# Attention of a two-layer transformer trunk: where the maxima stand between the scores, and the reciprocal in two halves

## The chip, the cores and the metric

One core of a Trainium2 chip runs the whole kernel. The metric is device time in microseconds for one execution, the median of several runs. TensorE (PE) does the matmuls, VectorE (DVE), ScalarE (ACT) and GpSimd (POOL) the rest, SyncE (SP) issues the transfers.

## The reference

A trunk of two layers over 1024 latent tokens and 256 context tokens, 1024 wide. Layer 0 mixes tokens by grouped-query attention (16 heads of 64, 4 key heads), layer 1 by latent attention (16 heads, 96 wide for the scores, 64 for the values); each mixer is followed by a gated feed-forward part. What the change touches is the attention:

```
s = einsum('bqhgd,bkhd->bhgqk', q, k) * scale
p = softmax_f32(s)
o = einsum('bhgqk,bkhd->bqhgd', p, v)
```

Queries are the latent tokens, keys and values context and latent tokens (1280). In layer 0 the context tokens attend to themselves as well.

## The kernel before, in words

All matmuls of large operands are made of 2 or 3 passes over a high and a low part of each operand. Everything is transposed: channels or keys on the partitions, tokens in the columns.

Attention works in units: a pair of heads by 512 queries, 16 units per layer (and in layer 0 eight small context units of 256 queries on the side). A unit goes over the 1280 keys in ten blocks of 128. In `Attention.run` (line 789) each block k does this: `scores` (line 661) writes the scores of both heads, 512 columns each, into a two-bank PSUM tile `psD` (two of those); ScalarE's exponential writes them to a tile `pt` of 1024 columns; GpSimd adds `pt` to the unit's running sum (block 1 goes to VectorE); and after every second block `flush` (line 796) multiplies the `pt` of two earlier blocks by the values into a bank `psB`. Layer 0 has 2 passes per head in `scores`, layer 1 has 3.

The softmax needs a maximum for each query ahead of the unit's scores. `unit_max` (line 617) works it out: 20 steps per unit, each a 512-column matmul (or two of 256) into a bank `psB` and a `reduce_max` of that bank by VectorE. After the last step VectorE takes the maximum over the three parts (`m`), ScalarE and VectorE write its two 16-bit parts (`mm`), and `max_row` (line 650) turns them into two rows beside the queries, so that the next unit's scores come out with the maximum subtracted. The steps of a unit are spread over the blocks of the unit before and the one before that: behind each block, up to three steps are taken while their number is under what is due, which rises by two per block.

A finished unit goes through `tail` (line 688): the value sums are copied from their bank, two matmuls with a matrix of ones add up the running sum over the partitions into another bank `psB` (this is done at the head of the next flush), VectorE takes the reciprocal of that bank in place and multiplies it with the copied values (`s<-psB,s`), and the product is stored. Since TensorE's next maxima need VectorE to free their banks, `tail` sets `em.calm`: no step is taken for 2.8 us behind the reciprocal.

There are four banks `psB`. The maxima, the value sums, the sums for the reciprocal, the projections of queries and keys and the maximum rows all use them.

The order of the work is made on the host. A class `Emitter` holds a planned time `em.now`; each matmul adds its planned cost (in `mm`, 512 columns at 2400 per us plus 0.0135), and side tasks written as generators yield the planned time after which they go on. They run inside a matmul's tick, except in a flush, which is emitted alone (`em.alone`, line 144); what falls due in it follows behind it. Inside attention every engine keeps this order (`pinned`).

Of the kernel before, what the change touches and what calls it, by code (L numbers as in the profile page):

```python
# [25 lines left out]
EPS = 1e-6  # L26

MROW_WAIT = 5.0
CALM = 2.8
PO_WAIT = 0.3  # L30
PACE0 = 0.5
STEPS = 20
# [129 lines left out]
def build(ctx, tc, A, out):  # L162
# [17 lines left out]
    pe, act, dve, pool = Engine("pe", nc.tensor), Engine("act", nc.scalar), Engine("dve", nc.vector), Engine("pool", nc.gpsimd)  # L180
    em = Emitter()
# [29 lines left out]
    def s4(dt=F32):  # L211
        return bp.tile([P, 1024], dt, tag="s4", name=nm("s4"), bufs=8)
# [6 lines left out]
    def ptile():  # L219

        tag, pool_, n = ptags["order"][ptags["next"] % len(ptags["order"])]
        ptags["next"] += 1
        return pool_.tile([P, 1024], F32, tag=tag, name=nm("pt"), bufs=n)

    def s2(dt=F32):
        return bp.tile([P, 512], dt, tag="s2", name=nm("s2"), bufs=5)

    def pD():
        return ps.tile([P, 1024], F32, tag="D", name=nm("psD"), bufs=2)

    def pB():
        return ps.tile([P, 512], F32, tag="B", name=nm("psB"), bufs=4)
# [13 lines left out]
    def mm(o, l, r, start=True, stop=True, tp=None, more=False):  # L246

        n = r.shape[-1]
        if r.dtype == F32:
            c = max(4 * n, 4 * l.shape[-1]) / 2400.0 * (1.0 if tp is None else 0.5 if l.shape[-1] == 64 else 0.28)  # L250
        elif r.dtype == F32R:
            c = n / 2400.0 + em.over
        else:
            c = 0.06
        if tp is None:
            pe.matmul(o, l, r, start=start, stop=stop, skip_group_check=more)
        else:
            pe.matmul(o, l, r, start=start, stop=stop, tile_position=tp)
        em.tick(c)
# [81 lines left out]
    def mm3(o, wh, wl, xh, xl, first=True, last=True, more=False):  # L341
        mm(o, wh, xh, first, False, more=more)
        mm(o, wh, xl, False, False, more=more)
        mm(o, wl, xh, False, last, more=more)
# [313 lines left out]
        u["ready"] = True  # L658
        yield 0.0

    def scores(u, S, kc):
        nq = u["nq"]
        for h in range(2):
            passes = u["passes"][h]
            for j, (k, q) in enumerate(passes):
                mm(S[:, h * nq:(h + 1) * nq], k[:, kc * P:(kc + 1) * P], q, j == 0, j == len(passes) - 1)

    def weigh(u, po, pt, kc, first, last):
        nq = u["nq"]
        for h in range(2):  # L670
            mm(po[64 * h:64 * h + 64, :nq], u["v"](h, kc), pt[:, h * nq:(h + 1) * nq], first, last, tp=(0, 64 * h))
# [5 lines left out]
    def run_jobs():  # L677
        while jobs:
            jobs.pop(0)()

    def post(job):

        if gather[0]:
            jobs.append(job)
        else:
            job()

    def tail(u, po, acc):
        nq = u["nq"]
        yield PO_WAIT  # L690
        o = s2()
        act.copy(o[:, :nq], po[:, :nq])
        res = {}

        def total():
            pss = res["pss"] = pB()
            for h in range(2):
                mm(pss[64 * h:64 * h + 64, :nq], ones, acc[:, h * nq:(h + 1) * nq], tp=(0, 64 * h))

        post(total)  # L700
        while not res:
            yield 0.3
        yield 1.0
        r = res["pss"][:, :nq]
        dve.reciprocal(r, r)
        em.calm = em.now + CALM * nq / 512
        yield 3.5 * nq / 512
        dve.tensor_tensor(o[:, :nq], r, o[:, :nq], ALU.mult)
        yield 1.2
        u["out"](o[:, :nq])  # L710
        u["done"] = True

    def ctx_unit(make, scale):
# [11 lines left out]
        for i, kc in enumerate((8, 9)):  # L725
            S = pB()
            scores(u, S, kc)
            pt = t[:, 2 * nq * i:2 * nq * (i + 1)]
            act.activation(pt, S[:, :2 * nq], AF.Exp, scale=scale)
            pts.append(pt)  # L730
            yield 1.0
# [10 lines left out]
        while not res:  # L742
            yield 0.3
        yield from tail(u, res["po"], acc)

    class Attention:
# [42 lines left out]
        def run(self, extra=None):  # L789
            em.spawn(self.prep(1))  # L790
            pend, adds = [], []
            gather[0] = self.inside = True
            pinned.update(ENGINES)
            em.over = 0.0135

            def flush(n):
                with em.alone():
                    run_jobs()
                    for _ in range(min(n, len(pend))):
                        u, po, pt, i = pend.pop(0)  # L800
                        if i == 0:
                            po[0] = pB()
                        weigh(u, po[0], pt, i, i == 0, i == 9)
                        if i == 9:
                            em.spawn(tail(u, po[0], u["acc"]))

            def add(u, pt, i):
                if i == 0:
                    u["p0"] = pt
                    return  # L810
                eng = dve if i in (LASTDVE if u is self.units[-1] else ACCD) else pool
                if i == 1:
                    u["acc"] = s4()
                    eng.tensor_tensor(u["acc"], u.pop("p0"), pt, ALU.add)
                else:
                    eng.tensor_tensor(u["acc"], u["acc"], pt, ALU.add)

            for i, u in enumerate(self.units):
                while "ready" not in u:
                    if self.steps >= (i + 1) * STEPS:  # L820
                        em.until(lambda: "ready" in u)
                    elif not next(self.max):
                        em.until(lambda t=em.now: em.now > t)
                if i + 2 < self.n:
                    em.spawn(self.prep(i + 2), 1.0)
                if extra:
                    extra(i)
                po = [None]
                for k in range(10):
                    S = pD()  # L830
                    scores(u, S, k)
                    pt = ptile()
                    act.activation(pt, S, AF.Exp, scale=self.scale)
                    while adds:
                        add(*adds.pop())
                    adds.append((u, pt, k))
                    pend.append((u, po, pt, k))
                    for _ in range(3):
                        if (em.now >= em.calm and self.steps < (i + 1) * STEPS + STEPS // 2 + 2 * (k + 1)
                                and not next(self.max)):  # L840
                            break
                    if len(pend) == BATCH + LEAD:
                        flush(BATCH)
            add(*adds.pop())
            while pend:
                flush(BATCH)
            pinned.difference_update(ENGINES)
            em.over = 0.0
            gather[0] = False
            run_jobs()  # L850
# [70 lines left out]
    class Up:  # L921
# [61 lines left out]
        def step(self, c, n, k):  # L983
            s = self.st[c]
            wn, xn = self.PR[n]
            w = self.ops[c][wn]
            wh, wl = w[:, k * P:(k + 1) * P], w[:, 512 + k * P:512 + (k + 1) * P]
            first = k == 0
            if n in ("V1", "V2", "G1", "G2"):
                o = s["ct"][:, 0:256] if n[0] == "V" else s["ct"][:, 256:512]  # L990
                kk = k + xn
                em.until(lambda: self.norm.ready(NX, kk))
                mm3(o, wh, wl, self.H["hh"][kk][:, NX:NT], self.H["hl"][kk][:, NX:NT], first and n[1] == "1",
                    k == 3 and n[1] == "2")
                return
            if n == "P1" and first:
                s["d"] = pD()
                s["a"], s["b"], s["ct"] = s["d"][:, 0:512], pB(), s["d"][:, 512:1024]
            if n in ("P2", "Q1") and first:
                s["x"] = pB()  # L1000
            o = s["b"] if n in ("P5", "P3") else s["x"] if n in ("P2", "Q1", "Q2") else s["a"]
            em.until(lambda: self.need(xn, k))
            xh, xl = self.mov(xn, k)
            more = n in ("P6", "P7", "P4", "P3")
            mm3(o, wh, wl, xh, xl, first and not more and n != "Q2", k == 3 and n != "Q1", more)
# [80 lines left out]
        def ahead(self):  # L1086
# [9 lines left out]
            self.ops[0]["go"] = True  # L1096

        def run(self, tail):
            em.until(lambda: "go" in self.ops[0])
            ctx = self.full  # L1100
# [1030 lines left out]
```

## Time and profile before

| what | us |
|---|---|
| median of 3 runs | 3445.76 |
| lowest and highest of them | 3443.13, 3451.75 |
| the profiled execution's own time | 3444.86 |
| its span, first to last instruction | 3443.1 |

The profile is of one execution. Times in it count from its first instruction. A matmul's duration is longer than the distance to the next matmul, because they are pipelined; the distance is what counts for a sum. Since nearly all instructions are recorded from one helper line (L175), the rows are told apart by the tiles that an instruction writes and reads, as `mx<-psB` for a reduction of a bank into the table of maxima.

### The profile page before, as it was taken

The page shows a single profiled execution, that of the slowest core. Times are in us where ns is not written, and L with a number is a line of the kernel's source. Part 1 is how long each engine was busy: PE and PEld are TensorE (multiplying, and loading weights), DVE is VectorE, ACT ScalarE, POOL GpSimd, SP SyncE. Part 2 cuts the span into 40 slices and gives each one's busy share as a digit, 9 for nine tenths or more (in the row PEclk, how much of TensorE's full clock was granted, in tenths as well). Part 3 has the DMA queues.
Part 4 walks back from the last instruction along what each step waited for, and adds up shares of the span by engine and source line. Part 5 has one row for each costly group of instructions (what it writes and reads, how often), then busy time and mean ns, then how long its engine had stood idle before and what let it go on. Part 6 is the DMA issues. An engine that isn't in the chain of part 4 may idle for free. (4 is left out here: it accounts for less than half of the span.)

```text
span 3443.1 us, 41383 instructions
## 1 busy us (share of the span) xinstructions
PE 3204.6 (93%) x15482; PEld 2342.0 (68%) x15482; DVE 2134.5 (62%) x2577; ACT 1520.2 (44%) x2368; POOL 1909.7 (55%) x1128
## 2 busy tenths in 40 slices
PE   6999999999989999999899899999999899998998
PEld 4776445556778888878777555555557677776787
DVE  5355766763576676667764655555553776767585
ACT  4224555552344444444453444444442444444434
POOL 4324667774466666654443355555562656566455
PEclk9999999999999999999999999999999899999998
DMA  5645310002312222264231000000014122223633
GB/s 199 196 146 188 111 59 8 19 1 89 103 49 78 84 97 86 69 216 149 82 114 60 23 28 11 28 11 28 19 49 140 44 92 92 92 92 119 236 113 101
DMA packets 139050, 303.33 MB, mean 88 GB/s; under 512 B 15584, under 2 KB 35168, under 8 KB 138848
## 3 DMA queue, kind: packets, MB, share of 16 engines
q1 hardware_dynamic: 138848, 300.67, 26.2%
q8 instruction: 122, 2.00, 0.2%
q14 instruction: 80, 0.66, 0.1%
HBM read 224.85 MB, written 70.52 MB: 86 GB/s over the span
## 5 line engine op out<-in xcount | busy, mean ns | idle before, releaser
L175 POOL TENSOR_TENSOR s<-s,pt 128x1024 f32<-128x1024 f32 x248 | 594.6, 2398 | 257.1 <-ACT pt L175 238.2
L175 DVE TENSOR_REDUCE mx<-psB 128x1 f32<-128x512 f32 (+1 forms) x640 | 407.5, 682 | 247.8 <-PE psB L175 246.0
L175 PE MATMUL psD<-s,blk 128*128 128x512 f32 (+2 forms) x1600 | 453.3, 410 | 3.9 <-ACT s L175 2.7
L175 ACT ACTIVATE pt<-psD 128x1024 f32<-128x1024 f32 x320 | 327.0, 1023 | 293.8 <-PE psD L175 281.0
L175 PEld LDWEIGHTS psD<-s,blk 128*128 128x128 f32 (+2 forms) x1600 | 289.4, 191 | 179.4 <-issue 73.8
L175 PE MATMUL psD<-blk,wh 128*128 128x512 f32 (+1 forms) x1024 | 335.0, 403 | 9.6 <-ACT blk L175 4.0
L175 DVE SCALAR_TENSOR_TENSOR s<-s,par,s 128x1023 f32<-128x1023 f32 x176 | 291.5, 1670 | 68.4 <-ACT s L175 65.2
L175 PE MATMUL psB<-pt,blk 128*64 128x512 f32 x1280 | 323.2, 627 | 0.3 <-DVE s L175 0.3
L175 PE MATMUL psD<-blk,wlo 128*128 128x512 f32 (+1 forms) x1398 | 287.9, 354 | 30.9 <-POOL wlo L175 22.2
L175 PE MATMUL psD<-blk,pp 128*128 128x512 f32 (+1 forms) x1068 | 268.5, 395 | 19.9 <-ACT pp L175 10.8
L175 PEld LDWEIGHTS psD<-blk,wlo 128*128 128x128 f32 x1398 | 229.7, 190 | 78.1 <-POOL wlo L175 30.6
L175 PE MATMUL psB<-blk,s 128*128 128x512 f32 (+3 forms) x768 | 231.6, 384 | 45.2 <-DVE mx L175 33.9
L175 PE MATMUL psB<-blk,pp 128*128 128x512 f32 x1056 | 262.0, 396 | 3.6 <-DVE s L175 2.7
L175 DVE TENSOR_TENSOR s<-s,s 128x512 f32<-128x512 f32 (+3 forms) x193 | 197.2, 1024 | 89.5 <-ACT s L175 75.6
L175 DVE TENSOR_TENSOR pp<-pp 128x512 fp32r<-128x512 f32 (+1 forms) x165 | 145.4, 889 | 166.2 <-ACT pp L175 164.4
L175 PEld LDWEIGHTS psD<-blk,pp 128*128 128x128 f32 x1068 | 199.5, 191 | 63.8 <-ACT pp L175 12.1
L175 POOL TENSOR_TENSOR pp<-wraw,pp 128x512 fp32r<-128x512 f32 x88 | 144.9, 1647 | 171.8 <-ACT pp L175 171.8
L175 PEld LDWEIGHTS psD<-blk,wh 128*128 128x128 f32 (+1 forms) x1024 | 188.8, 189 | 74.7 <-issue 17.5
L175 POOL TENSOR_TENSOR s<-s,s 128x1024 f32<-128x1024 f32 (+4 forms) x72 | 143.8, 2001 | 170.0 <-ACT s L175 165.9
L175 PEld LDWEIGHTS psB<-blk,pp 128*128 128x128 f32 x1056 | 198.9, 191 | 50.6 <-DVE s L175 7.2
L175 PEld LDWEIGHTS psB<-blk,s 128*128 128x128 f32 (+1 forms) x768 | 141.3, 193 | 110.0 <-DVE mx L175 66.8
L175 POOL TENSOR_TENSOR whi<-blk,whi 128x512 fp32r<-128x512 f32 x97 | 143.8, 1483 | 127.8 <-ACT whi L175 123.1
(159 smaller groups left out, 6025.4 us busy)
## 6 DMA issues: line engine op xcount, KB each, us to landing
pp<-g SPq DMA_DIRECT2D x143, 256.0 KB, 2.8
g<-s SPq DMA_DIRECT2D x66, 512.0 KB, 2.7
s<-in_ada_w SPq DMA_DIRECT2D x48, 512.0 KB, 5.8
blk<-in_ada_w SPq DMA_DIRECT2D x48, 512.0 KB, 6.4
wraw<-in_w_up SPq DMA_DIRECT2D x88, 256.0 KB, 3.0
pp<-in_w_up SPq DMA_DIRECT2D x88, 256.0 KB, 3.9
blk<-in_w_dn SPq DMA_DIRECT2D x86, 256.0 KB, 3.4
wr<-in_w_out SPq DMA_DIRECT2D x16, 512.0 KB, 3.8
```

Of the source, the lines that this page charges most:

```text
L175: ins = fn(*a, **k)
```

## The change

In `scores` a function may be called between the two heads. `run` hands it one step of the maxima, if fewer than due less one are done. Behind the exponential's emission, in place of up to three steps, comes one step if fewer than due are done and a second if fewer than due less one are; and one more is possible behind a flush. A step is taken only when the planned time is past `em.calm`, as before. The reciprocal of 512 columns becomes two of 256 (the context units' of 256 stays one), each sets a calm of 1.0 us instead of 2.8 (1.4 for 256), and the task waits 2.3 planned us behind each instead of 3.5 (1.75) behind the whole.

```diff
 MROW_WAIT = 5.0
-CALM = 2.8
+CALM = 1.0
+RECW = 2.3
@@
-    def scores(u, S, kc):
+    def scores(u, S, kc, between=None):
         nq = u["nq"]
         for h in range(2):
+            if h and between:
+                between()
             passes = u["passes"][h]
             for j, (k, q) in enumerate(passes):
                 mm(S[:, h * nq:(h + 1) * nq], k[:, kc * P:(kc + 1) * P], q, j == 0, j == len(passes) - 1)
@@
         r = res["pss"][:, :nq]
-        dve.reciprocal(r, r)
-        em.calm = em.now + CALM * nq / 512
-        yield 3.5 * nq / 512
+        for a in range(0, nq, 256):
+            dve.reciprocal(r[:, a:a + 256], r[:, a:a + 256])
+            em.calm = em.now + CALM
+            yield RECW
         dve.tensor_tensor(o[:, :nq], r, o[:, :nq], ALU.mult)
@@
+            def step(due):
+                if em.now >= em.calm and self.steps < due:
+                    next(self.max)
+
             for i, u in enumerate(self.units):
@@
                     S = pD()
-                    scores(u, S, k)
+                    due = (i + 1) * STEPS + STEPS // 2 + 2 * (k + 1)
+                    scores(u, S, k, lambda: step(due - 1))
                     pt = ptile()
                     act.activation(pt, S, AF.Exp, scale=self.scale)
                     while adds:
                         add(*adds.pop())
                     adds.append((u, pt, k))
                     pend.append((u, po, pt, k))
-                    for _ in range(3):
-                        if (em.now >= em.calm and self.steps < (i + 1) * STEPS + STEPS // 2 + 2 * (k + 1)
-                                and not next(self.max)):
-                            break
+                    step(due)
+                    step(due - 1)
                     if len(pend) == BATCH + LEAD:
                         flush(BATCH)
+                        step(due)
```

## Rows read from the trace of the kernel before

**Rows 1.** The page's busy line, whole execution: busy us (share of the span) xinstructions.

```profile
PE 3204.6 (93%) x15482; PEld 2342.0 (68%) x15482; DVE 2134.5 (62%) x2577; ACT 1520.2 (44%) x2368; POOL 1909.7 (55%) x1128
```

**Rows 2.** Windows: length, busy PE, PEld, DVE, ACT, POOL, granted clock, DMA, GB/s.

```profile
290.00:805.00 515.00, 481.58 (x2228) 248.82 (x2229) 355.31 (x467) 277.91 (x396) 372.09 (x180) 0.98 0.18 63
1940.00:2540.00 600.00, 559.70 (x2449) 344.98 (x2449) 328.41 (x447) 258.92 (x369) 337.72 (x172) 0.96 0.07 22
2124.90:2130.00 5.10, 4.97 (x22) 2.85 (x23) 3.31 (x6) 2.48 (x4) 0.00 (x0) 1.00 0.00 0
2150.40:2153.80 3.40, 3.40 (x9) 1.04 (x9) 1.72 (x3) 0.00 (x0) 1.72 (x1) 0.50 0.00 0
```

**Rows 3.** The waits of TensorE's matmuls, 290 to 800 us: total, times, longest.

```profile
PE psB L175 <- DVE mx L175: 18.9, 32, 2.3
...
PE psB L175 <- DVE m L175: 1.8, 6, 0.4
```

**Rows 4.** The same view, 1940 to 2600 us.

```profile
PE psB L175 <- DVE mx L175: 22.3, 15, 2.9
PE psB L175 <- DVE blk L175: 7.8, 8, 1.2
PE psB L175 <- DVE s L175: 5.3, 4, 1.7
```

**Rows 5.** The timeline around the end of a flush: start, duration, idle before.

```profile
2137.67 1.91 PE L175 MATMUL psB<-pt,blk 128*64 128x512 f32 x8
...
2138.60 3.36 DVE L175 RECIPROCAL psB<-psB 128x512 f32<-128x512 f32 x1
...
2139.51 0.72 PE L175 MATMUL psD<-s,blk 96*128 96x512 f32 x2
```

**Rows 6.** The timeline of the same unit, 6 us later.

```profile
2144.87 7.25 POOL L175 TENSOR_TENSOR s<-s,pt 128x1024 f32<-128x1024 f32 x3
...
2145.89 0.85 PE L175 MATMUL psB<-blk,s 96*128 96x512 f32 x4
...
2146.32 1.29 DVE L175 TENSOR_REDUCE mx<-psB 128x1 f32<-128x512 f32 x2 [3.64 <-PE psB L175]
...
2146.58 1.56 PE L175 MATMUL psD<-s,blk 96*128 96x512 f32 x6
2147.64 0.18 DVE L175 TENSOR_REDUCE m<-mx 128x8 f32<-128x24 f32 x1
...
2147.97 0.63 PE L175 MATMUL psB<-blk,s 96*128 96x512 f32 x2
2148.10 1.63 DVE L175 SCALAR_TENSOR_TENSOR mm<-m,mm 128x8 bf16<-128x8 f32 x1 [0.28 <-ACT mm L175]
...
2150.38 0.80 PE L175 MATMUL psB<-blk,s 96*128 96x512 f32 x1 [1.78 <-DVE mx L175]
...
2151.11 3.27 PE L175 MATMUL psB<-pt,blk 128*64 128x512 f32 x8
```

**Rows 7.** The timeline of a unit of layer 1 with values to prepare.

```profile
2057.34 3.37 DVE L175 RECIPROCAL psB<-psB 128x512 f32<-128x512 f32 x1
...
2061.49 1.09 PE L175 MATMUL psB<-wh,blk 128*128 128x256 f32 x4 [1.66 <-DVE s L175]
```

**Rows 8.** Groups of VectorE instructions (busy, mean ns), and one tile's durations (min/median/max).

```profile
L175 DVE RECIPROCAL psB<-psB 128x512 f32<-128x512 f32 x32 | 107.4, 3355 | 35.5 <-PE psB L175 34.5 <-ACT s L175 0.9
L175 DVE RECIPROCAL psB<-psB 128x256 f32<-128x256 f32 x7 | 12.3, 1758 | 0.3 <-PE psB L175 0.2
L175 DVE TENSOR_REDUCE mx<-psB 128x1 f32<-128x512 f32 x240 | 155.5, 679 | 61.0 <-PE psB L175 60.1
L175 DVE SCALAR_TENSOR_TENSOR mm<-m,mm x40: 150/882/2248, 238.2 to 2563.5; 128x8 bf16<-128x8 f32 x32, 128x4 bf16<-128x4 f32 x8
```

**Rows 9.** The timeline of a unit of layer 0, around its reciprocal.

```profile
605.20 3.35 DVE L175 RECIPROCAL psB<-psB 128x512 f32<-128x512 f32 x1
...
608.47 0.62 DVE L175 TENSOR_REDUCE mx<-psB 128x1 f32<-128x512 f32 x1
```

## The prediction

> **What bounds the kernel now.** I read the page's busy line first: TensorE is busy for 93% of the span and no other engine for more than 62% [rows 1], so time is lost or won where TensorE waits or is slow. Two stretches hold everything the change touches, the attention of layer 0 (290 to 805 us) and of layer 1 (about 1900 to 2600 us). The windows view gives their granted clock [rows 2]: 0.98 and 0.96 of full speed, and 0.50, that is 1.2 instead of 2.4 GHz, in the 3.4 us that follow one wait. Over the 600 us of the second row 0.04 are 24 us lost to the clock; one drop of 3.4 us at half speed loses 1.7 us, so there are some thirteen drops.
>
> Next I read whom TensorE's matmuls waited for. In layer 0 it is the maxima on VectorE: 18.9 us in 32 waits, and 1.8 us for the final maximum [rows 3]. In layer 1 the maxima stand for 22.3 us in 15 waits, and a VectorE operation on "s" for 5.3 us in 4, the longest 1.7 us [rows 4]. The timeline shows what one of them is [rows 5, 6]. The planner bans maxima for 2.8 us behind the reciprocal, then lets three go behind each block, here four matmuls from 2145.89 on (two whole steps and one of two halves). The last maximum of the unit ends with a tiny VectorE operation "mm" on 8 columns that takes 1.63 us here, because it ends (2149.73) as GpSimd's running add ends. The reductions behind it are late, no PSUM bank is free, and the matmul at 2150.38 has waited 1.78 us. Behind it come the eight value matmuls in 3.27 us, at 1.2 GHz [rows 2, 6]; the same eight take 1.91 us at full clock [rows 5]. In a unit in four it looks different [rows 7]: the whole reciprocal (3.37 us) stands before the last maxima, and the wait is 1.66 us for the product "s" behind it. So an event costs 1.78 + 1.7 = 3.5 us; 27.6 us of waits in layer 1 are room for at most fifteen, and I count twelve, one for each drop but one. At stake in layer 1: 12 x 3.5 = 42 us.
>
> **The change, part by part.** It removes nothing but the three steps in a row. No matmul, DMA or queue is added or moved; what moves is where 20 maxima per unit stand in TensorE's and VectorE's order, and each of 32 full reciprocals becomes two.
>
> The halves. A 512-column reciprocal takes 3355 ns, one of 256 columns (the context units have them already) 1758 ns [rows 8]: 2 x 1758 - 3355 = 161 ns more per unit, 32 times, 5.2 us of VectorE. VectorE works 355 of 515 us in layer 0 and 328 of 600 in layer 1 [rows 2], and I cost this at nothing; without that cover it is 5.2 us. [...]
>
> The order, by the planner's costs (0.227 us for a 512-column matmul; 1.71 us for a flush, in which nothing else is emitted). Call F the end of the flush in the fourth block of a layer-1 unit; the tail emits the reciprocal 1 us behind it. New order: maximum 19 between the heads of the fifth block, half A, maximum 20 (the unit's last, with "mm") between the heads of the sixth, 21 behind it, flush. Half B is due at 1.13 + 2.3 = 3.4 us, inside the flush, so it is emitted behind that, bans maxima for 1 us, and 22 and 23 follow behind the seventh block, 24 between the heads of the eighth. Two per block, never three.
>
> Now with measured times, F = 2139.51 [rows 5]: six score matmuls take 1.39 us (2146.58 to 2147.97), the flush 1.84, a reduction starts 0.43 after its matmul and takes 0.68 [rows 6, 8]. Reduction 19 ends at F + 1.8; half A, which starts 2.7 us later than the reciprocal today (2138.60, F - 0.9), F + 3.6; reduction 20 F + 4.3; "mm" is ready 0.46 after the final maximum starts, at F + 4.7. GpSimd runs its adds back to back; one ends at 2144.87 = F + 5.4 [rows 6], and "mm" slips in there. Reduction 21 ends at 6.1, half B at 7.9, reduction 22 at 8.6. Matmul 24 is wanted at F + 7.9 and needs the bank of 22: two of the four banks of "psB" are held by the value sum and by the reciprocal's sums until the product. It waits 0.7 us where one waited 1.78: 12 x 1.08 = 13 us gained. The waits of up to 1.2 us on "blk" in layer 1 [rows 4] leave the clock where it was: behind one of them, from 2124.9 on, 1.00 was granted [rows 2]. So a wait of 0.7 should keep it; as the units with weights to prepare may differ from this one, I count nine of twelve, 9 x 1.7 = 15.3 us. Bounds for layer 1: all twelve stay (0) and all waits and drops go (27.6 + 20.4 = 48 us); nearest is the timetable. What is late next behind this wait is the exponential that gives the score tile back: a maximum between the heads delays it by 0.23 us, and ScalarE, busy 259 of 600 us [rows 2], hides that.
>
> Layer 0. A block has 4 score matmuls, so the fifth and sixth are through sooner and half B's ban reaches over the seventh. One maximum goes between A's block, none till the eighth, then eleven in three blocks. Today the reciprocal starts at 605.20, and one maximum waits behind it and is reduced at 608.47 [rows 9]. In the new order nothing stands between the halves, and A starts behind the maximum. But the steps are split by heads and flush, and where three follow a block today, blocks away from a reciprocal get two. I take half of 18.9 + 1.8, 10 us; bounds 0 and 20.7. The clock's 0.02 x 515 = 10 us I leave, bounds 0 and 10.
>
> Later ends. The product comes at 2 x 2.3 instead of 3.5 planned us, 1.1 later; behind each layer's last unit the projection starts with other units' outputs, so nothing waits.
>
> **Sum:** 13 + 15.3 + 10 = 38 us off the profiled execution's 3444.86 us: 3406.6. That execution lies 0.9 us below the median 3445.76, so 3407.
>
> **Rivals.** A, slower: "mm" misses the gap at F + 5.4 and waits for the next add, 2.4 us on. In place it decides all: reduction 21 ends at 8.5, matmul 23 waits 1.5 us for it; half B and reduction 22 follow at 10.9, matmul 24 waits another 1.5. That is 3.0 in place of 1.78, with the drop kept: 16 x 1.2 = 19.5 us more in layer 1, and half that in layer 0: 3445 + 29 = 3474. The margin is 5.4 - 4.7 = 0.7 us; against it speaks that the boundary repeats with the unit, for it that "mm" ranges from 150 to 2248 ns [rows 8]. [...]
>
> B, no change: the same wait appears one block earlier, with the same length, since the bank shortage stays: 3441, within 10 us of before.
>
> C, it doesn't do in layer 0 what it says: no maximum falls between half A and half B there, VectorE is held by both as by the whole, and nothing is won: 38 - 10 = 28 us, 3417.
>
> **The numbers.** Chances: forecast 0.50, A 0.14, B 0.14, C 0.22. A measurement of this kernel can tell about 0.3%, 10.3 us. Forecast and C are faster (0.72), B the same (0.14), A slower (0.14). The range goes from all of layer 1's and layer 0's waits gone with twelve drops (48 + 20.7 = 69, 3377) to B's far edge (3445.8 + 10.3 = 3456); A lies outside. The forecast and C alone span 3377 to 3430.
>
> **What would show it.** Right: layer 1's granted clock near 0.99; matmul waits on maxima there under 12 us; halves of 1.76 us with a reduction between them in layer 1; no block with three maxima in a row behind its scores. Wrong: "mm" at 1.6 us or more with a TensorE wait behind it in most units, the clock still 0.96, or new waits of the score matmuls on the exponentials.

## The result, and the profile of the changed kernel

The changed kernel takes 3405.49 us (median of 4 runs, 3404.28 to 3410.3), the kernel before 3444.45 us (4 runs, 3430.03 to 3451.75). The ratio on record is 0.9902 with the interval 0.9882 to 0.9921; the quotient of the two medians is 0.9887 and lies inside it. The total is the forecast's to within 2 us. Its split is not, as the windows show.

The head of the page and its busy line, after:

```profile
span 3402.8 us, 41374 instructions
...
PE 3169.4 (93%) x15482; PEld 2333.4 (69%) x15482; DVE 2163.1 (64%) x2609; ACT 1517.1 (45%) x2368; POOL 1902.4 (56%) x1128
```

Against [rows 1], VectorE has 32 instructions more (2609 for 2577), the second halves, and TensorE is 35.2 us less busy with the same 15482 matmuls. Most of that is its clock: the mean granted clock of the execution was 0.970 before and 0.977 after, and 0.007 of 3443 us are 24 us.

The windows from the first to the last exponential of each layer's attention and the stretch between them, first of the kernel before, then of the changed one (length, busy PE, PEld, DVE, ACT, POOL, granted clock, DMA, GB/s):

```profile
289.00:793.30 504.30, 474.05 (x2206) 245.68 (x2208) 345.69 (x460) 277.19 (x393) 366.53 (x179) 0.98 0.19 64
793.30:1953.90 1160.60, 1099.24 (x5633) 920.13 (x5630) 747.18 (x867) 513.98 (x867) 599.35 (x399) 0.97 0.28 95
1953.90:2595.00 641.10, 600.54 (x2609) 364.56 (x2609) 347.64 (x457) 278.30 (x385) 375.88 (x186) 0.96 0.08 26
```

```profile
289.70:805.70 516.00, 474.11 (x2212) 244.32 (x2212) 376.04 (x478) 275.67 (x393) 361.68 (x179) 0.98 0.19 64
805.70:1961.80 1156.10, 1095.06 (x5631) 920.47 (x5632) 746.94 (x867) 514.08 (x867) 595.97 (x399) 0.98 0.28 94
1961.80:2556.40 594.60, 572.65 (x2603) 359.26 (x2603) 345.29 (x471) 276.06 (x385) 376.22 (x186) 0.99 0.08 28
```

Layer 1 gained 641.1 - 594.6 = 46.5 us. Of these, 18.6 us are idle time of TensorE (length less busy: 40.6 before, 22.0 after) and 27.9 us busy time. Layer 0 **lost** 516.0 - 504.3 = 11.7 us, all of it idle time (30.3 before, 41.9 after) at an unchanged clock. The stretch between gained 4.5 us, whose cause was not sought. The sum is 39.3 us of the 40.3 us between the two profiled executions (3444.86 and 3404.57).

The inner part of layer 1 in the windows view of the changed kernel:

```profile
1980.00:2500.00 520.00, 505.13 (x2335) 320.09 (x2334) 306.75 (x428) 240.02 (x342) 329.04 (x165) 1.00 0.07 24
```

The clock is 1.00 there: none of the twelve drops to a granted 0.50, of which [rows 2] show one, is left. Two longer drops stand outside this row, at the ends of the layer (granted 0.50 from 1964.8 to 1971.6 us and from 2507.5 to 2514.3). The prediction's 1.2 and 2.4 GHz can be estimated, as columns per ns, from starts in the kernel before. In the drop of [rows 2] two pairs of value matmuls start at 2152.02 and 2152.87 us, 0.85 us for 1024 columns: 1.2. At full clock twelve matmuls of 512 columns take 2.72 us (1213.31 to 1216.03) and twelve of 256 right behind them 1.43 (to 1217.46), so 3072 columns more take 1.29 us more: 2.4. Below, TensorE's waits after, in layer 0 (290 to 800 us; total, times, longest) and in layer 1 (1965 to 2600 us):

```profile
PE psB L176 <- DVE mx L176: 28.4, 33, 3.0
```

```profile
PE psB L176 <- DVE mx L176: 13.4, 18, 4.4
PE psB L176 <- DVE blk L176: 5.7, 4, 2.1
PE psB L176 <- DVE s L176: 2.2, 4, 0.6
```

The waits on maxima rose in layer 0 from 18.9 to 28.4 us [rows 3]. In layer 1 they fell from 22.3 to 13.4 us [rows 4], of which one wait, at 2509 us in the last unit but one, is 4.4 us.

**Layer 1: the timetable held.** The timeline of a layer-1 unit after, with F = 2095.35 as the end of the flush in its fourth block (start, duration, idle before):

```profile
2095.35 0.96 PE L176 MATMUL psD<-s,blk 96*128 96x512 f32 x3
...
2096.59 0.69 DVE L176 TENSOR_REDUCE mx<-psB 128x1 f32<-128x512 f32 x1 [3.03 <-PE psB L176]
...
2097.19 1.75 DVE L176 RECIPROCAL psB<-psB 128x256 f32<-128x256 f32 x1
...
2098.51 4.88 POOL L176 TENSOR_TENSOR s<-s,pt 128x1024 f32<-128x1024 f32 x2 [1.75 <-ACT pt L176]
...
2098.86 0.63 DVE L176 TENSOR_REDUCE mx<-psB 128x1 f32<-128x512 f32 x1
...
2099.98 0.92 DVE L176 SCALAR_TENSOR_TENSOR mm<-m,mm 128x8 bf16<-128x8 f32 x1 [0.28 <-ACT mm L176]
...
2100.82 0.68 DVE L176 TENSOR_REDUCE mx<-psB 128x2 f32<-128x512 f32 x1
...
2101.42 1.75 DVE L176 RECIPROCAL psB<-psB 128x256 f32<-128x256 f32 x1
...
2103.09 1.21 DVE L176 TENSOR_REDUCE mx<-psB 128x1 f32<-128x512 f32 x2
...
2104.22 0.68 DVE L176 TENSOR_TENSOR s<-psB,s 128x512 f32<-128x512 f32 x1
2104.36 0.50 PE L176 MATMUL psB<-blk,s 96*128 96x512 f32 x1 [0.20 <-DVE mx L176]
```

"mm" is ready at F + 4.6 and ends at F + 5.55, as the first of the two adds in GpSimd's row ends (2098.51 plus half of 4.88 is 2100.95). So it still ends with an add, but sooner: it takes 0.92 us where it took 1.63 [rows 6]. Matmul 24 waits 0.20 us where one waited 1.78.

**Layer 0: the bank of the sums came back too late.** The timeline of the layer-0 unit of [rows 9], after:

```profile
607.19 1.08 PE L176 MATMUL psB<-s,ones 128*64 128x512 f32 x4
...
611.38 0.69 DVE L176 TENSOR_REDUCE mx<-psB 128x1 f32<-128x512 f32 x1 [1.73 <-PE psB L176]
...
611.99 1.76 DVE L176 RECIPROCAL psB<-psB 128x256 f32<-128x256 f32 x1
...
613.73 7.31 POOL L176 TENSOR_TENSOR s<-s,pt 128x1024 f32<-128x1024 f32 x3
613.78 2.60 DVE L176 TENSOR_TENSOR blk<-blk,blk 64x256 fp32r<-64x256 f32 x1
...
616.30 1.75 DVE L176 RECIPROCAL psB<-psB 128x256 f32<-128x256 f32 x1
...
618.64 0.50 PE L176 MATMUL psB<-blk,s 128*128 128x512 f32 x1 [1.50 <-DVE mx L176]
...
619.08 1.98 DVE L176 SCALAR_TENSOR_TENSOR mm<-m,mm 128x8 bf16<-128x8 f32 x1 [0.28 <-ACT mm L176]
...
621.58 0.67 DVE L176 TENSOR_TENSOR s<-psB,s 128x512 f32<-128x512 f32 x1
621.81 0.47 PE L176 MATMUL psB<-blk,blk 128*128 128x256 f32 x2 [0.80 <-DVE mx L176]
```

Read it as the life of one of the four "psB" banks. The sums are written into it from 607.19 on, and only the product that ends at 622.25 gives it back: 15.1 us. Before it was 6.5 us in this unit, from 603.30 to 609.82, with the reciprocal in between at 605.20 [rows 9]:

```profile
603.30 1.08 PE L175 MATMUL psB<-s,ones 128*64 128x512 f32 x4 [0.19 <-DVE mx L175]
...
609.13 0.69 DVE L175 TENSOR_TENSOR s<-psB,s 128x512 f32<-128x512 f32 x1
```

After, half A stands behind the next block's maximum, which TensorE delivers late (1.73 us idle). Between the halves comes a subtraction of 64x256, which takes 2.60 us and ends (616.38) about as GpSimd's first add of three does (613.73 + 7.31/3 = 616.17). Then half B, the last maximum and "mm", which ends (621.06) as the third add does (621.04); the product stands last. TensorE waits for a bank twice, 1.50 and 0.80 us.

This is no accident of one unit. Of the 31 "mm" of 128x8 in the two layers, 16 took over 0.7 us before and 23 after, and each of these 39 ended within 0.04 us of the end of a GpSimd instruction. The seven subtractions that took over 0.7 us after ended 0.28 to 0.29 us behind one. What ties these ends to each other was not shown.

The groups view of VectorE in layer 0 (290 to 805 us; busy, mean ns), before and then after, gives the sums:

```profile
L175 DVE SCALAR_TENSOR_TENSOR mm<-m,mm 128x8 bf16<-128x8 f32 x15 | 7.8, 518 | 4.2 <-ACT mm L175 4.2
L175 DVE TENSOR_TENSOR blk<-blk,blk 64x256 fp32r<-64x256 f32 x11 | 4.6, 419 | 0.1
```

```profile
L176 DVE TENSOR_TENSOR blk<-blk,blk 64x256 fp32r<-64x256 f32 x11 | 18.0, 1640 | 0.2
L176 DVE SCALAR_TENSOR_TENSOR mm<-m,mm 128x8 bf16<-128x8 f32 x15 | 16.1, 1073 | 4.5 <-ACT mm L176 4.5
```

The same eleven subtractions went from 419 to 1640 ns each, "mm" from 518 to 1073 ns: 13.4 + 8.3 = 21.7 us more of VectorE for the same work in another order.

### The profile page after: what moved, and what is told of

Read it like the earlier page. It is cut to its first block, busy times and chain, and to the rows that moved or that the text cites. A ratio compares the mean times of both kernels' runs of the same rounds, so it can differ in the third digit from the quotient of the medians.

```text
span 3402.8 us, 41374 instructions
## 1 busy us (share of the span) xinstructions
PE 3169.4 (93%) x15482; PEld 2333.4 (69%) x15482; DVE 2163.1 (64%) x2609; ACT 1517.1 (45%) x2368; POOL 1902.4 (56%) x1128
## 5 line engine op out<-in xcount | busy, mean ns | idle before, releaser
L176 POOL TENSOR_TENSOR s<-s,pt 128x1024 f32<-128x1024 f32 x248 | 592.4, 2389 | 224.9 <-ACT pt L176 126.5
L176 DVE TENSOR_REDUCE mx<-psB 128x1 f32<-128x512 f32 (+1 forms) x640 | 420.7, 682 | 228.4 <-PE psB L176 226.3
L176 PE MATMUL psD<-s,blk 128*128 128x512 f32 (+2 forms) x1600 | 483.3, 408 | 4.5 <-ACT s L176 3.3
L176 PE MATMUL psD<-blk,wlo 128*128 128x512 f32 (+1 forms) x1398 | 287.2, 353 | 31.0 <-POOL wlo L176 22.3
L176 PE MATMUL psB<-pt,blk 128*64 128x512 f32 x1280 | 311.0, 607 | 2.4 <-ACT pt L176 1.0
L176 PE MATMUL psB<-blk,s 128*128 128x512 f32 (+3 forms) x768 | 263.2, 381 | 30.1 <-DVE mx L176 21.7
L176 PE MATMUL psD<-blk,pp 128*128 128x512 f32 (+1 forms) x1068 | 268.6, 395 | 21.3 <-ACT pp L176 12.0
```

Of the source, the lines that this page charges most:

```text
L176: ins = fn(*a, **k)
```

## The experiments

"Layer 0" and "layer 1" below are the times from the first to the last exponential of each layer's attention in the profiled execution; before they are 503.3 and 640.1 us, after 515.0 and 593.6. Two profiles of a layer with the same order differ by up to some 6 us, as shown below, so smaller differences of these times are not read as effects. The kernel before took 3437.36 us beside the first four kernels (12 runs), 3439.6 beside the next four (7 runs) and 3439.12 beside the last two (7 runs).

### Which of the two parts does it, and in which layer

**The new places alone.** The maxima stand as in the change; the reciprocal is whole again, with its old ban and wait.

```diff
-CALM = 1.0
+CALM = 2.8
@@
-        for a in range(0, nq, 256):
-            dve.reciprocal(r[:, a:a + 256], r[:, a:a + 256])
-            em.calm = em.now + CALM
-            yield RECW
+        dve.reciprocal(r, r)
+        em.calm = em.now + CALM * nq / 512
+        yield 3.5 * nq / 512
```

> The new places of the maxima with the whole reciprocal of before and its calm of 2.8. Theory S (the three steps in a row make layer 1's waits and clock drops): layer 1's attention, 640 us before and 594 after, is at most 605, its granted clock 0.98 or more, and the kernel 3405 to 3415. Rival H (the halves let maxima through): layer 1 stays at 630 to 640 with 0.96, and the kernel within 10 us of before. Both: layer 0 tells whether the halves or the places cost the 12 us there, 503 against 515 us from the first exponential to the last.

Measured: 3406.82 us, ratio 0.9909 (0.9894 to 0.9923); layer 0 507.7, layer 1 598.0. That is the change's total, without the halves. Between 1980 and 2500 us it leaves two drops of the clock, near 2212 and 2369 us, where a matmul waits for the product behind a whole reciprocal, as in [rows 7]. The timeline and the window behind the first of them:

```profile
2211.95 2.63 PE L176 MATMUL psB<-wh,blk 128*128 128x256 f32 x12 [1.68 <-DVE s L176]
```

```profile
2212.50:2216.00 3.50, 3.50 (x16) 2.65 (x17) 1.23 (x4) 0.86 (x3) 2.82 (x2) 0.53 0.20 75
```

The halves end these two in the change (the waits on "s" are 2.2 us there, none over 0.6), which is some 4 us of layer 1, and layer 0 is 7.3 us longer with them. In the kernel's time the two nearly cancel. In layer 0 the halves move TensorE's waits from the product to the maxima: with the whole reciprocal (289.6 to 798.4 us) they are

```profile
PE psB L176 <- DVE mx L176: 14.6, 19, 3.6
PE psB L176 <- DVE s L176: 9.6, 8, 3.2
```

and with the halves 28.4 us on maxima and 1.4 us on "s".

**The halves alone.** The order of the maxima is the old one, up to three behind each block; the reciprocal is the change's. The edit, against the kernel before:

```diff
-CALM = 2.8
+CALM = 1.0
+RECW = 2.3
@@
-        dve.reciprocal(r, r)
-        em.calm = em.now + CALM * nq / 512
-        yield 3.5 * nq / 512
+        for a in range(0, nq, 256):
+            dve.reciprocal(r[:, a:a + 256], r[:, a:a + 256])
+            em.calm = em.now + CALM
+            yield RECW
```

> The two halves with calm 1.0 and 2.3 us behind each, but up to three steps behind each block as before. Theory S: layer 1 keeps most of its drops, clock 0.96 to 0.97, attention 625 to 640 us, the kernel 3430 to 3445. Rival H: layer 1 at 594 to 605 us, the kernel 3405 to 3415.

Measured: 3424.85 us, ratio 0.9963 (0.9948 to 0.9978); layer 0 516.7, layer 1 614.7 at a clock of 0.99 (1.00 between 1980 and 2470 us). Neither expectation holds as written. The halves alone take the drops away too and win 25.4 of 46.5 us in layer 1; they cost 13.4 us in layer 0. So the two parts don't add up: either one keeps the clock in most units of layer 1, and the old order keeps waits that the new one doesn't have (20.3 us on maxima in layer 1 against 13.4). The trace gives the reason why the halves alone do it. The durations of layer 1's "mm" (shortest, median, longest in ns), before and with the halves alone:

```profile
L175 DVE SCALAR_TENSOR_TENSOR mm<-m,mm x15: 171/1615/1626, 1977.8 to 2563.5; 128x8 bf16<-128x8 f32 x15
L176 DVE SCALAR_TENSOR_TENSOR mm<-m,mm x15: 170/209/2012, 1986.9 to 2543.9; 128x8 bf16<-128x8 f32 x15
```

The old order still lets three maxima follow a block, but half of the "mm" take 209 ns or less, where half took 1615 or more, and the waits on maxima are shorter: 28 of 0.7 us on average where before 15 of 1.5 us stood. The waits for the product, too, are 2.2 us with none over 0.6, as in the change.

**The change in layer 1 only, and in layer 0 only.** A flag, set as each attention starts, picks the old or the new order and reciprocal. Only the line that sets it is shown; 0.125 is layer 0's scale.

```diff
+            newway[0] = self.scale != 0.125
```

> The whole change in layer 1, layer 0 as before. Theory: layer 0's part is a loss of its own, 12 us, so 3405 - 12 = 3393, faster than both kernels. Rival: what layer 0 loses in attention comes back behind it (the stretch from its end to layer 1 was 4.5 us shorter after), so 3400 to 3405.

Measured: 3395.94 us, ratio 0.9874 (0.9859 to 0.9889); layer 0 504.5, layer 1 593.2.

```diff
+            newway[0] = self.scale == 0.125
```

> The whole change in layer 0, layer 1 as before. Theory: 12 us slower than before, 3452 to 3460, and layer 1's clock 0.96 as before. Rival (layer 1 gains because its start is shifted, not by its own order): layer 1 at 600 us here too, and the kernel under 3425.

Measured: 3448.7 us (9 runs), ratio 1.0027 (1.0015 to 1.0039); layer 0 514.1, layer 1 638.3. That is 11.3 us over the kernel before beside it, for 12 expected. The two layers can be told apart cleanly: layer 1's part alone is faster than the whole change, and layer 0's part is a loss of its own.

### What makes the events of layer 1

**The kernel before without VectorE's "mm".** The old order and the whole reciprocal stay. "mm" splits the negated maximum into two 16-bit columns, ScalarE the first, VectorE the rest. Here ScalarE writes half of it into both, and VectorE does nothing.

```diff
-        act.mul(mb[:, :w, 0], m[:, :w], -1.0)
-        dve.scalar_tensor_tensor(mb[:, :w, 1], m[:, :w], -1.0, mb[:, :w, 0], ALU.mult, ALU.subtract)
+        act.mul(mb[:, :w, 0], m[:, :w], -0.5)
+        act.mul(mb[:, :w, 1], m[:, :w], -0.5)
```

> The kernel before, with the tiny VectorE operation on mm replaced: ScalarE writes minus half the maximum into both 16-bit columns, so that their sum is the maximum rounded to 16 bits. The shift is a little coarser, which softmax does not see. Theory M (the wait of mm for GpSimd's add makes nine of the twelve events of layer 1): those nine go, three drops with the reciprocal stay; layer 1's attention falls from 640 to 605 to 618 us, and the kernel by 20 to 35 us. Rival S (three steps in a row are enough by themselves to run out of banks): waits of about 1 us stay in each unit, drops go or stay, layer 1 at 625 or more, the kernel within 15 us of before.

Measured: 3393.1 us, ratio 0.9864 (0.9849 to 0.988); layer 0 494.0, layer 1 604.0. This one edit is worth 46 us, more than the change and more than the 20 to 35 expected (layer 1 gains 36.1 us, and layer 0, which the theory left out, 9.3); and it leaves the three steps in a row where they were. TensorE's waits in layer 1 of this kernel (1940 to 2600 us):

```profile
PE psB L175 <- DVE blk L175: 8.7, 8, 1.2
PE psB L175 <- DVE s L175: 5.3, 4, 1.7
...
PE psB L175 <- DVE mx L175: 3.4, 4, 2.9
```

The waits on maxima went from 22.3 to 3.4 us, and the granted clock to 0.99; the waits on "blk" and "s" stayed about as in [rows 4]. Of the twelve drops two are left, near 2202 and 2363 us, behind waits for the product (up to 1.7 us). This shows what the prediction read from [rows 6]: the three steps were not the trouble by themselves, but a tiny operation in VectorE's queue ahead of two reductions. That it is long because it waits for a GpSimd add is read from the ends of the long ones, as above; no run moved the adds instead.

**The same edit on the kernel that has the change in layer 1 only.**

> The change in layer 1 alone (3396 us) and also ScalarE writing both 16-bit columns, in both layers. Theory: in layer 1 mm ran 0.8 to 0.9 us and its wait was hidden, so little is left there (0 to 5 us); in layer 0 the waits on maxima behind mm (1.8 us of TensorE waits on m, and part of 18.9 on mx) shrink by 3 to 8 us: 3384 to 3393. Rival (mm sets nothing any more): 3393 to 3398.

Measured: 3387.6 us, ratio 0.9845 (0.9828 to 0.9861); layer 0 488.4, layer 1 592.4. In layer 1 the edit gives 0.8 us more beside the new order (593.2 without it): both remove the same events. In layer 0, where the old order still has waits behind "mm", it gives 16.1 us here and 9.3 us in the kernel before. Both have the same order there, so two single profiles of a layer can differ by some 6 us.

### What costs in layer 0

**The reciprocal first.** The new places, the whole reciprocal as in the first experiment, and it is emitted without the planner's microsecond behind the sums.

```diff
             yield 0.3
-        yield 1.0
         r = res["pss"][:, :nq]
```

> The new places with the whole reciprocal (3407 us, layer 0 508 us), but the reciprocal is emitted at the end of the flush, ahead of the next block's maximum. Theory B (layer 0 loses because the reciprocal now stands behind a maximum of the next block, and its bank of sums is held the longer): layer 0 at 498 to 504 us, the kernel 3395 to 3403. Rival (the order of the reciprocal and that maximum is of no weight; the places themselves cost): layer 0 at 506 to 510 us, the kernel 3404 to 3409.

Measured: 3382.47 us, ratio 0.9833 (0.9813 to 0.9853); layer 0 486.4, layer 1 594.2. Layer 0 gains 21.3 us over the first experiment, more than the theory expected (498 to 504 us). The timeline of the same unit as above in this kernel:

```profile
587.64 1.08 PE L176 MATMUL psB<-s,ones 128*64 128x512 f32 x4
...
590.02 3.36 DVE L176 RECIPROCAL psB<-psB 128x512 f32<-128x512 f32 x1
...
594.40 0.69 DVE L176 TENSOR_TENSOR s<-psB,s 128x512 f32<-128x512 f32 x1
```

The reciprocal starts 2.4 us behind the first matmul of the sums, where half A started 4.8 us behind it (611.99 - 607.19), and the bank is back after 7.45 us (595.09) instead of 15.1. Over the sixteen units of layer 0 the mean of that time is 13.6 us in the change, 11.6 with the new places alone and 8.3 here, in the order of layer 0's times (515.0, 507.7, 486.4).

The bank's time is not all, though. In the kernel before its mean is 7.6 us, the shortest of these, and layer 0 takes 503.3 us. So with the bank held for about as long the new places win 16.9 us in layer 0 (503.3 to 486.4); the reciprocal's late start takes back 21.3 and the change's halves on top of it 7.3 more. The halves in the old order agree: 11.8 us and 516.7, where the new places have 507.7 at 11.6. In layer 1 a longer hold cost nothing that can be seen: its mean is 11.6 us in the change and 6.5 here, for 593.6 and 594.1 us.

**Both halves, back to back.** The change, but with no wait between the halves and the old ban and wait behind them.

```diff
-            em.calm = em.now + CALM
-            yield RECW
+        em.calm = em.now + 2.8 * nq / 512
+        yield 3.5 * nq / 512
```

> The change, but the second half stands right behind the first on VectorE, with the calm of 2.8 us and the 3.5 us of the whole behind both. Theory G (the 7 us that the change loses in layer 0 against the same places with a whole reciprocal come from the gap between the halves, in which other VectorE work slips in and the bank of sums stays held): layer 0 at 506 to 510 us, the kernel 3404 to 3410, as with the whole reciprocal. Rival F (a fixed cost of two instructions): layer 0 at 513 us or more.

Measured: 3406.45 us, ratio 0.9905 (0.9884 to 0.9926); layer 0 508.3, layer 1 597.0, within 1 us of the whole reciprocal in the same places (507.7 and 598.0). To split the instruction costs nothing that can be seen; what the halves cost in layer 0, they cost through the gap between them, or through the shorter ban on maxima that goes with it: this edit takes both back, and no run tells them apart. Each side was profiled twice: 515.0 and 514.1 us with the gap, 507.7 and 508.3 without.

**The halves first.** The change itself without the planner's microsecond (the same line goes as above).

> The change, with the first half emitted at the flush's end, ahead of the next block's maximum; the second 2.3 planned us later, calm 1.0 behind each. Theory: with the first half early the product still waits for the second, so layer 0 lies between 486 us (whole, first) and 515 (the change): 490 to 505, the kernel 3385 to 3398. Rival (the halves let maxima through, as they are meant to): layer 0 at 486 us or less and the kernel at 3382 or less.

Measured: 3396.07 us, ratio 0.9881 (0.9862 to 0.99); layer 0 507.3, layer 1 594.4. Started early, the halves are still 20.9 us longer in layer 0 than the whole reciprocal started as early (486.4), and longer than the 490 to 505 us expected. So the two prices don't add up either: over 486.4 us the late start alone costs 21.3 us, the halves alone 20.9 and both together, in the change, 28.6. The medians of the two kernels lie 13.6 us apart (3396.07 and 3382.47). TensorE's waits on maxima there are about 21 us here and 14 us with the whole one first.

### The version that beats both

**New places, whole reciprocal first, no "mm" on VectorE.**

> New places, the whole reciprocal emitted at the flush's end (3382 us), and ScalarE writing both 16-bit columns. Theory: the two gains touch different waits in layer 0 (the bank of sums; reductions behind mm), so part of the 9 us that the second one brought to layer 0 before adds: layer 0 at 478 to 484 us, layer 1 at 590 to 594, the kernel 3368 to 3380. Rival (both remove the same waits): 3380 to 3386.

Measured: 3371.18 us (3367.89 to 3371.36), ratio 0.9806 (0.9786 to 0.9826); layer 0 471.1, layer 1 594.1. That is 68 us less than before, and by the two ratios (0.9902 - 0.9806) 33 us less than the change. Layer 0 was expected at 478 to 484 us and came out better. Without "mm" on VectorE, too, the new places with the early reciprocal win 17 to 23 us in layer 0 over the old order (488.4 and 494.0 to 471.1). TensorE's waits on maxima in layer 0 (290 to 762.1 us) are a third of before's 18.9 us:

```profile
PE psB L176 <- DVE mx L176: 6.2, 9, 1.6
```

## Why the prediction was right, and where it was not

- **The cause in layer 1: right, and shown.** The drops end, all or all but two, with the order, with the halves, or with "mm" alone taken away. What the prediction took from [rows 6] as the source, "mm" behind an add, is the one whose removal needs nothing else.
- **The timetable: right.** Predicted and measured behind F: reduction 19 ends at 1.8 and 1.9 us, half A at 3.6 and 3.6, reduction 20 at 4.3 and 4.1, "mm" ready at 4.7 and 4.63, the add's end at 5.4 and 5.6, reduction 21 at 6.1 and 6.1, half B at 7.9 and 7.8. That "mm" slips in there is what rival A denied; its wait for the next add came in one unit of fifteen in layer 1 (1.77 us).
- **The size of layer 1's terms: too small.** 13 us of waits measured 18.6 us of idle time; in the unit shown the wait of matmul 24 became 0.20 us and not 0.7. (The 13 us took twelve waits for maxima; three of the twelve events had a wait for the product, as [rows 7].) Nine of twelve drops at 1.7 us (15.3 us) became twelve of twelve (20.4 us); TensorE's busy time fell by 27.9 us, and the 7.5 us beyond that were not traced further (the drop at 1964.8 us, some 3.4 us by half its length, even goes against it). Together 46.5 for 28, close to the upper bound of 48. The sign it had set for itself, under 12 us of waits on maxima in layer 1, was missed by the one wait of 4.4 us near the layer's end; the others make 9.0.
- **The step that failed is layer 0's.** "I take half of 18.9 + 1.8, 10 us; bounds 0 and 20.7" measured a loss of 11.7 us, below its lower bound: a loss was left out without a reason to exclude it. The gain that it counts on is there, 16.9 us with the reciprocal first and whole. What it lacks is the price of the bank that comes back late, 28.6 us by the experiments, and behind that stand three sentences. "A starts behind the maximum" was seen and priced at nothing; a late start alone costs 21.3 us. "In the new order nothing stands between the halves" looked only at maxima; the 64x256 subtraction stands there, and the halves alone cost 20.9 us. And "The product comes [...] 1.1 later; [...] so nothing waits" looked at who reads the product, not at the bank that the product gives back, although the same text had named that bank among the two held. In the unit shown the bank was held 8.6 us longer (15.1 for 6.5), over the layer's sixteen units 6.0 us (13.6 for 7.6).
- **The rivals.** C, nothing won in layer 0, was nearer than the forecast's term, and in the unit shown no maximum falls between the halves, as it says; A's late "mm" that ends with an add did come, but near the 2.4 us of an add only in layer 0 (up to 2.38 us there, 1.77 in layer 1). B's "same wait one block earlier" did not.
- **The cost of the split: right.** Costed at nothing, with 5.2 us as the price without cover: the halves back to back took 3406.45 us, the whole 3406.82.
- **The total was right by compensation.** Layer 1 gave 18 us more than forecast, layer 0 22 us less, and the stretch between 4.5 us that nobody had forecast.
- **Open.** That the subtraction alone makes the cost of the gap in layer 0 wasn't tried; the gap and the shorter ban are shown together. Why a late bank costs so much in layer 0 and nothing that can be seen in layer 1 wasn't tried either.

## What to carry to other kernels

When a stall repeats, ask of the last instruction in the chain not how long it is but what it waits for and who stands behind it: eight columns on VectorE, given to ScalarE, gained 46 us, a reordering of the whole attention 39. An operation that gives back a scarce buffer can be worth starting early and finishing in one go, even if something else is late by its length (here 21.3 us in layer 0, nothing that can be seen in layer 1); a gap inside it is filled by whatever stands next in the engine's order, and that may itself take long (here the subtraction of 64x256, 1.64 us on average). And when a term is bounded, name the buffers that a later end holds, not only the readers of the result.

## What the hardware showed that was not expected

- How long small VectorE operations take hangs on where they stand: the same eleven subtractions of 64x256 in layer 0 take 419 ns on average in one order and 1640 ns in another, "mm" from 0.15 to 2.4 us.
- The clock does not drop behind every wait of this length. In the kernel before, TensorE waited 1.77 us near the end of layer 1, as long as in [rows 6], and the eight value matmuls behind took 1.94 us (1.91 in [rows 5]), with the clock granted at 1.00 from 2524.6 to 2531 us. The timeline of TensorE there:

```profile
2524.41 0.63 PE L175 MATMUL psB<-blk,s 96*128 96x512 f32 x2
2526.80 0.50 PE L175 MATMUL psB<-blk,s 96*128 96x512 f32 x1 [1.77 <-DVE mx L175]
2527.23 1.94 PE L175 MATMUL psB<-pt,blk 128*64 128x512 f32 x8
```

In layer 1 of the kernel with the reciprocal first, even 2.38 us passed without a drop. The timeline there, and the window behind the wait with the clock granted at 1.00:

```profile
2192.29 1.69 PE L176 MATMUL psB<-wh,blk 128*128 128x256 f32 x12 [2.38 <-DVE s L176]
```

```profile
2192.30:2195.70 3.40, 3.40 (x22) 3.10 (x23) 1.97 (x4) 0.65 (x2) 3.26 (x2) 1.00 0.22 82
```

So the length of one wait does not decide it alone; what else does wasn't settled here.
